# Where the value products of the band pairs stand in TensorE's order: odd pairs first in their turn, even pairs last

## The chip, the cores and the metric

The kernel runs on one core of a Trainium2 chip. The core has a matrix engine (TensorE, PE in the profile; its weight loads are shown as PEld), VectorE (DVE), ScalarE (ACT), GpSimd (POOL) and a sync engine (SP) that issues most DMAs. Each engine works through its own queue, and the queues are tied together by semaphores. TensorE writes its results to PSUM, from where ACT and DVE read them. The metric is the time of one execution in device microseconds, as the median of several runs.

## What is computed

The reference is a two-layer encoder trunk on 1024 tokens of width 1024. Each layer has 16 attention heads of width 64 in three groups, an output projection and a gated feed-forward part. The change touches the attention of the groups A and B, whose scores lie in a band around the diagonal:

```python
for l in range(DEPTH):                                  # DEPTH = 2
    h = rms_norm(x, g_attn[l]) * (1 + sc_a) + sh_a
    qa, ka, va, qb, kb, vb, qc, kc, vc = split_cols(h @ w_in[l], IN_SPLITS)
    ya = neighborhood_attention(qa, ka, va, rpb_na[l])                   # 4 heads
    yb = sliding_window_attention(qb, kb, vb, sink_sw[l], t5_table)      # 6 heads
    yc = axial_attention(qc, kc, vc, gq_ax[l], gk_ax[l])                 # 6 heads, dense
    y = concat(rms_norm(ya, ga), rms_norm(yb, gb), rms_norm(yc, gc))
    x = x + gt_a * (y @ w_o[l])
    ...                                                  # feed-forward part

# sliding window, per 128-query block, against the 3 blocks of keys around it:
s = einsum('bnqgrd,bnkgd->bngrqk', qb, kb) * scale + bias
p = softmax(concat([s, sink_logits]))[..., :-1]
o = einsum('bngrqk,bnkgd->bnqgrd', p, vb)
```

## The kernel before

The attention of one layer is a stream of 64 pairs. A pair is one head with 256 queries (two blocks of 128), numbered p = 0 to 3 within a head. Pairs 0 to 23 are the dense group C (class `PairC`), pairs 24 to 39 are group A (`PairA`) and 40 to 63 are group B (`PairB`); A and B are both `Band`, and they are what the change touches.

A band pair goes through these steps:

- `scores` (line 1571): four products on TensorE into a PSUM tile (sA or sB in the profile; two buffers of two banks each), then two instructions on DVE that add the bias and take the maximum into `pr`.
- `exps` (line 1592): two exponentials on ACT, in place in `pr`.
- `divide` (line 1600): a reciprocal on DVE and two scalings on POOL.
- `turn` (line 1603): four transposes into one PSUM bank and one or two into another (both named T; three banks in all), then a cast on ACT of the first bank to the high part (`pt<-T`) and a copy of the second (`edge<-T`). `low` puts the low part together on DVE from the first bank (also `pt<-T,pt`).
- `pv` (line 1624): the value products, four with the two parts of `pt` and two or four hardware products with `edge`, into the PSUM tile pv.
- `fold` (line 1431) and `combine` (line 1440), for odd p only: ACT copies 64 rows of pv to the tile cmb, and DVE adds them to the other rows and writes y.

The pv tile holds two pairs: an even pair writes its left half and the odd pair after it the right half, and both are folded together. `psV` has `4 - PS_T` banks, and PS_T is 3, so there is one bank for pv (line 1361). An even pair therefore may not begin `pv` before `combine` of the odd pair ahead of it has read the bank.

The loop at line 1767 runs over turns n. In the band part (its last branch, line 1794) a turn works on several pairs at once: `divide` for n + 2, `low` of n - 1, `combine` of n - 3, `scores` of n + 4, `exps` of n + 3, `turn` of n, `pv` and `fold` of n - 2. Where this text says an odd or an even turn it means the parity of n, which is that of the pair whose `pv` and `turn` it holds. While `pin` is on (line 1876), TensorE, ACT, DVE and POOL keep exactly the order in which the code writes their instructions; the work in `later` and what stands below line 1822 (norm statistics, scalings of y, splits of the output projection's weights) is placed by the scheduler. All engine calls go through one helper, so that every row of the profile has its line, L49, and rows are told apart by their tiles.

Of the kernel before, what the change touches and what calls it, by code (L numbers as in the profile page):

```python
# [85 lines left out]
def trunk(ctx: ExitStack, tc, A, C, out):  # L86
# [5 lines left out]
    def pin(engines, on):  # L92
        for e in engines:
            e.pinned = on
# [103 lines left out]
    def w_rows(w, r0, hl=None, eng=None):  # L198

        return split_w(lambda v: [(v, w[r0 : r0 + P, :])], 1, hl, eng)  # L200
# [704 lines left out]
    for l in range(2):  # L905
# [14 lines left out]
        def qk_tile():  # L920
            return qkp.tile([P, 5, S], F32R, name="qk", tag="qk", bufs=2)
# [133 lines left out]
        def rows_A(i):  # L1055
            sp.dma_start(skA[i], bc(skr[4 * i : 4 * i + 4][:, None, :], [4, P, 512]))

        def rows_B():
            for h in range(6):
                sp.dma_start(skB[h], bc(rowB[h][None, :], [P, 512]))  # L1060
# [210 lines left out]
        def opened(p0, p1, p2, p3):  # L1271

            p0.turn(0)
            p2.dots(0)
            p0.turn(1)
            p2.dots(1)
            low = p1.turn_high(0, 0)
            p0.pv(0)
            p2.max(0)
            p2.exp(0)  # L1280
            low()
            low = p1.turn_high(0, 1)
            p0.pv(1)
            p2.max(1)
            low()
            low = p1.turn_high(1, 0)
            p2.exp(1)
            p3.dots(0)
            low()
            low = p1.turn_high(1, 1)  # L1290
            p1.pv(0)
            p3.max(0)
            unfinished.pop(0)()
            p3.exp(0)
            low()
            p3.dots(1)
            p1.pv(1, False)
            p1.fold()
            p3.max(1)
            p3.exp(1)  # L1300
            p1.combine()
# [172 lines left out]
        class PairC(Pair):  # L1474
# [8 lines left out]
            def max(self, c):  # L1483
                c_max(self.s[c], c, self.rs)
# [217 lines left out]
        def y_split(k, half, hi, lo):  # L1702

            c = slice(half * H, (half + 1) * H)
            g = vec[:, 64 + k : 65 + k]
            act.activation(hi, y[:, k, c], AF.Copy, scale=g)
            dve.scalar_tensor_tensor(
                out=lo, in0=y[:, k, c], scalar=g, in1=f32(hi), op0=ALU.mult, op1=ALU.subtract
            )
# [6 lines left out]
        def w_o_stage(k):  # L1716
            st = stage()
            sp.dma_start(st, w_o[k * P : (k + 1) * P, :])
            return st

        def o_rows(ki, w, ns):
            wh, wl = w
            if ki < 5:
                hi, lo = yq[:, ki, 0:H], yq[:, ki, H:S]
            else:
                hi, lo = yb[0][:, ki - 5, :], yb[1][:, ki - 5, :]
            for n in ns:
                cs = slice(n * P, (n + 1) * P)
                mm3(pss[n], wh[:, cs], wl[:, cs], hi, lo, ki == 0, ki == 7)
# [31 lines left out]
        N = len(stream)  # L1761
        pairs = {}
        AHEAD, AHEAD_B, NC = 3, 4, 24
# [3 lines left out]
        for n in range(-AHEAD - 1, N + 3):  # L1767
            ahead = AHEAD if n + AHEAD < NC else AHEAD_B
            begin = range(done, min(n + ahead + 1, N))
            if n < 0:  # L1770
                begin = range(done, done)
            elif n == 0:
                opened(*(pairs[i] for i in range(4)))
                begin = range(3, 4)
                fresh = []
            elif n < NC:
                for i in range(2 if n > 1 else 0):
                    if 0 <= n:
                        pairs[n].turn(i)
                    while unfinished:  # L1780
                        unfinished.pop(0)()
                    if 2 <= n - 1:
                        pairs[n - 1].pv(i)
                    for m in begin:
                        if m < min(made, NC):
                            pairs[m].qk(i)
                for i in range(2 if n == 1 else 0):
                    pairs[begin[0]].qk(i)
                fresh = [pairs[m] for m in begin if NC <= m < made]
                for b in fresh:  # L1790
                    b.scores()
                    b.exps()
                    b.divide()
            else:
                for b in worked:
                    b.divide()
                if NC <= n - 1 < N:
                    pairs[n - 1].low()
                if NC <= n - 3:
                    pairs[n - 3].combine()  # L1800
                fresh = [pairs[m] for m in begin if m < made]
                for b in fresh:
                    b.scores()
                for b in scored:
                    b.exps()
                if n < N:
                    pairs[n].turn()
                if NC <= n - 2 < N:
                    pairs[n - 2].pv()
                    pairs[n - 2].fold()  # L1810
                elif n == NC:
                    for i in range(2):
                        pairs[n - 1].pv(i)
                scored, worked = fresh, scored
            done = max(done, min(begin.stop, made)) if n >= 0 else done
            while made < min(N, n + ahead + 2):
                for key, make in preload.get(made, []):
                    heads[key] = make()
                pairs[made] = stream[made][0]()
                made += 1  # L1820
            if n >= 0:
                pin((pe, act, dve), False)
            for what in later.pop(n, []):
                what()
            if n in (0, 6):
                for j in range(8):
                    (v_back if n else v_store)(j)
            if n == 4 and l == 0:
                rows_A(1)
                rows_B()  # L1830
            if n == 6:
                pin((sp,), False)
            if n == 50:
                yq = qk_tile()
            if n == 54:
                wst = [w_o_stage(k) for k in korder[:2]]
            if n in (55, 59):
                ki = (n - 55) // 4
                y_split(korder[ki], 0, yq[:, ki, 0:H], yq[:, ki, H:S])
            if n in (59, 61):  # L1840
                w01.append(split_tile(wst.pop(0), 1, (atp, "pr", 6), dve))
            if n == 60:
                t2 = [psS.tile([P, 2, H], F32, name="ps_o", tag="S") for _ in range(2)]
                pss = [t2[i // 2][:, i % 2, :] for i in range(NS)]
            if n in (61, 62):
                o_rows(0, w01[0], range(NS)[2 * (n - 61) : 2 * (n - 60)])
            if n in (63, 64):
                o_rows(1, w01[1], range(NS)[2 * (n - 63) : 2 * (n - 62)])
            if n == 62:
                wq = [w_rows(w_o, k * P, eng=dve) for k in korder[2:4]]  # L1850
            m = n - 1 if n <= NC else n - 3
            for end, (chunks, width) in norms.items():
                if begins[end] <= m <= end and (m - begins[end]) % 8 == 7 and (n <= NC or m >= NC):
                    i = (m - begins[end]) // 8
                    if end not in gss:
                        gss[end] = gss_tile()
                    for half in range(2):
                        what = lambda a=(chunks, gss[end], i, half, m == N - 1): norm_sum(*a)
                        if m == N - 1:
                            what()  # L1860
                        else:
                            later.setdefault(n + 1 + half, []).append(what)
                    if m == end and end < N - 1:

                        def stats(end=end, width=width, n=n, chunks=chunks):
                            r = rstd_cols([gss[end]], width, 8, atp, psT, tag="T", newton=True)

                            def scale():
                                todo = norm_scale(chunks, r, psT, "T", (pool, pool))
                                for i, what in enumerate(todo):  # L1870
                                    later.setdefault(n + 9 + i, []).append(what)

                            later.setdefault(n + 8, []).append(scale)

                        later.setdefault(n + 5, []).append(stats)
            pin((pe, act, dve), n < 0 or n >= NC - 1)
# [713 lines left out]
```

## Time and profile before

| what | value |
|---|---|
| median of 3 runs | 2369.87 us (2369.44 to 2372.74) |
| the profiled execution's own time | 2368.57 us |
| its span | 2366.8 us |
| granted TensorE clock, mean | 0.998 |
| instructions | 33472 |
| first and last product into pv | 232.2 and 1628.0 us |
| VectorE, ScalarE, GpSimd: share of the span busy | 74%, 50%, 33% |

The bands of layer 0 run from about 359 to 454 us of the span and those of layer 1 from about 1549 to 1632 us. A row of the view in order of time reads: start in us, duration in us (of all instructions merged into the row), engine, line, operation, output<-inputs with shapes, count, and in brackets how long the engine had been idle before it and which instruction ended that. A row of the waits reads: who waited, for what, us in total, how many times, and the longest.

### The profile page before, as it was taken

What the parts mean: (1) busy time and instruction counts of PE and PEld (TensorE: products, weight loads), DVE (VectorE), ACT (ScalarE), POOL (GpSimd) and SP (SyncE); (2) the same over time, 40 slices, a digit from 0 to 9 for tenths busy, and PEclk for the clock granted to TensorE, in tenths of its full rate; (3) what the DMA queues carried; (4) which work ended last, traced back from release to release, by engine and by line L of the source; (5) the groups of instructions that cost most, each with busy time, mean ns of one, the idle gap of its engine ahead of it and who ended that gap; (6) DMA issues with size and microseconds to landing.
All of it is one profiled execution on the core that took longest, in us unless ns stands there. A gap on an engine that the chain in (4) does not pass through costs nothing. (4 is left out here: it accounts for less than half of the span.)

```text
span 2366.8 us, 33472 instructions
## 1 busy us (share of the span) xinstructions
PE 2325.0 (98%) x11804; PEld 1959.9 (83%) x11804; DVE 1756.6 (74%) x2753; ACT 1184.7 (50%) x2261; POOL 775.7 (33%) x747
## 2 busy tenths in 40 slices
PE   9999999999999999999999999999999999999998
PEld 7888898888788888788888889988878888888886
DVE  6877998869867677595767789897796674537765
ACT  4423888845543333344633168896454434334443
POOL 1530447610344445100145124574005444430001
PEclk9999999999999999999999999999999999999999
DMA  8667416162434444775434861332634443239633
GB/s 280 182 207 227 127 27 192 44 217 94 138 130 165 156 138 151 217 245 175 155 100 133 247 186 28 92 103 94 218 98 132 154 150 103 98 106 299 209 120 112
DMA packets 307417, 358.02 MB, mean 151 GB/s; under 512 B 51996, under 2 KB 223868, under 8 KB 307248
## 3 DMA queue, kind: packets, MB, share of 16 engines
q1 hardware_dynamic: 290752, 346.26, 46.4%
q10 hardware_dynamic: 16128, 9.44, 1.5%
q8 instruction: 93, 1.52, 0.3%
q14 instruction: 76, 0.62, 0.1%
q0 software_dynamic: 368, 0.17, 0.0%
HBM read 270.84 MB, written 88.63 MB: 152 GB/s over the span
## 5 line engine op out<-in xcount | busy, mean ns | idle before, releaser
L49 PE MATMUL ps_d<-wpt 128*128 128x512 f32 x1848 | 423.8, 390 | 1.0 <-ACT wpt L49 0.7
L49 PEld LDWEIGHTS ps_d<-wpt 128*128 128x128 f32 x1848 | 345.7, 188 | 74.4 <-issue 3.0
L49 POOL TENSOR_SCALAR pr<-pr,rs 128x1024 f32<-128x1024 f32 (+2 forms) x248 | 190.3, 780 | 186.2 <-DVE rs L49 169.7
L49 POOL TENSOR_TENSOR sg<-sg,u 128x512 f32<-128x512 f32 x82 | 118.0, 1440 | 348.4 <-ACT sg L49 221.6
L49 PE MATMUL pv<-pt,vs 128*128 128x256 f32 x1088 | 173.9, 296 | 14.6 <-DVE y L49 13.3
L49 DVE TENSOR_TENSOR pt<-T,pt 128x512 fp32r<-128x512 f32 x272 | 177.4, 680 | 7.0 <-ACT pt L49 5.9
L49 ACT CAST wpt<-w 128x512 fp32r<-128x512 f32 x154 | 95.7, 621 | 173.5 <-PE ps_d L49 155.3
L49 DVE SCALAR_TENSOR_TENSOR acc<-wmt,condT,acc 128x512 f32<-128x512 f32 (+1 forms) x98 | 117.0, 1202 | 77.7 <-DMA wmt<-in_w_mod_dram 77.2
L49 ACT CAST pt<-T 128x512 fp32r<-128x512 f32 x272 | 151.5, 585 | 42.0 <-PE T L49 40.7
L49 ACT COPY u<-ps_w 128x512 f32<-128x512 f32 x128 | 75.1, 586 | 192.9 <-PE ps_w L49 192.9
L49 POOL TENSOR_TENSOR wpt<-ws,wpt 128x512 fp32r<-128x512 f32 x80 | 111.2, 1390 | 182.2 <-ACT wpt L49 137.2
L49 DVE TENSOR_TENSOR wpt<-w,wpt 128x512 fp32r<-128x512 f32 x154 | 108.9, 707 | 79.2 <-ACT wpt L49 76.9
L49 PEld LDWEIGHTS pv<-pt,vs 128*128 128x128 f32 x1088 | 141.0, 189 | 27.2 <-DVE y L49 25.2
L49 PE MATMUL T<-identr,pr 128*128 128x128 f32 x1176 | 160.1, 273 | 0.9 <-ACT edge L49 0.5
L49 PEld LDWEIGHTS T<-identr,pr 128*128 128x128 f32 x1176 | 137.7, 140 | 16.0 <-issue 1.4
L49 ACT CAST wpt<-ws 128x512 fp32r<-128x512 f32 x176 | 107.7, 622 | 52.9 <-issue 22.9
L49 DVE TENSOR_TENSOR wpt<-graw,wpt 128x512 fp32r<-128x512 f32 x154 | 109.8, 713 | 16.6 <-ACT wpt L49 16.4
L49 ACT CAST wpt<-graw 128x512 fp32r<-128x512 f32 x154 | 95.0, 617 | 52.7 <-DMA graw<-gpd 43.6
L49 DVE TENSOR_TENSOR wpt<-ws,wpt 128x512 fp32r<-128x512 f32 x96 | 82.7, 869 | 49.3 <-ACT wpt L49 49.1
L49 DVE TENSOR_TENSOR ws<-wr 128x512 f32<-128x512 f32 x88 | 81.2, 923 | 50.0 <-POOL wpt L49 46.6
L49 DVE TENSOR_REDUCE rs<-sC 128x1 f32<-128x1024 f32 x88 | 107.4, 1221 | 12.7 <-PE sC L49 11.4
L49 PE MATMUL ps_w<-ht3h,wpt 128*128 128x512 f32 x352 | 108.8, 390 | 2.4 <-ACT sg L49 2.4
(306 smaller groups left out, 5931.5 us busy)
## 6 DMA issues: line engine op xcount, KB each, us to landing
wr<-in_w_gu_dram SPq DMA_DIRECT2D x92, 512.0 KB, 4.2
gpd<-sg SPq DMA_DIRECT2D x154, 256.0 KB, 4.4
graw<-gpd SPq DMA_DIRECT2D x76, 512.0 KB, 3.5
w<-in_w_down_dram SPq DMA_DIRECT2D x110, 256.0 KB, 5.4
wmt<-in_w_mod_dram SPq DMA_DIRECT2D x48, 512.0 KB, 5.9
qk<-qkd SPq DMA_DIRECT2D x44, 512.0 KB, 7.2
wst<-in_w_o_dram SPq DMA_DIRECT2D x32, 512.0 KB, 4.4
wmt<-in_w_mod_dram SPq DMA_DIRECT2D x64, 256.0 KB, 3.9
```

Source lines behind the costliest of these rows:

```text
L49: ins = op(*args, **kwargs)
```

## The change

In the band branch of the loop the pair whose value products belong to the turn (n - 2) is now called `ready`. If its p is odd, its `pv` is called ahead of the turn's scores; if its p is even, after the turn's transposes as before. `fold` is called where it was. Nothing else differs.

```diff
                 fresh = [pairs[m] for m in begin if m < made]
+                ready = pairs[n - 2] if NC <= n - 2 < N else None
+                if ready and ready.p % 2:
+                    ready.pv()
                 for b in fresh:
                     b.scores()
                 for b in scored:
                     b.exps()
                 if n < N:
                     pairs[n].turn()
-                if NC <= n - 2 < N:
-                    pairs[n - 2].pv()
-                    pairs[n - 2].fold()
+                if ready:
+                    if ready.p % 2 == 0:
+                        ready.pv()
+                    ready.fold()
                 elif n == NC:
                     for i in range(2):
                         pairs[n - 1].pv(i)
```

On TensorE, in the first head of group B in layer 0 (T are transposes, sB scores, pv value products), four turns read before:

```order
L49 MATMUL T<-identr,pr 128x128 x6
L49 MATMUL pv<-pt,vs 128x256 x4
L49 MATMUL pv<-edge,vs 128x128
L49 MATMUL sB<-qk 128x384 x4
L49 MATMUL T<-identr,pr 128x128 x6
L49 MATMUL pv<-pt,vs 128x256 x4
L49 MATMUL pv<-edge,vs 128x128
L49 MATMUL sB<-qk 128x384 x2
L49 MATMUL sB<-qk 128x256 x2
L49 MATMUL T<-identr,pr 128x128 x5
L49 MATMUL pv<-pt,vs 128x256 x4
L49 MATMUL pv<-edge,vs 128x128 x2
```

Every set of transposes is followed by one pair's value products: those of p = 3 (of the head before), p = 0 and p = 1 here.

The same place on TensorE after the change:

```order
L49 MATMUL pv<-pt,vs 128x256 x4
L49 MATMUL pv<-edge,vs 128x128
L49 MATMUL sB<-qk 128x384 x4
L49 MATMUL T<-identr,pr 128x128 x6
L49 MATMUL sB<-qk 128x384 x4
L49 MATMUL T<-identr,pr 128x128 x6
L49 MATMUL pv<-pt,vs 128x256 x4
L49 MATMUL pv<-edge,vs 128x128
L49 MATMUL pv<-pt,vs 128x256 x4
L49 MATMUL pv<-edge,vs 128x128 x2
L49 MATMUL sB<-qk 128x384 x2
L49 MATMUL sB<-qk 128x256 x2
```

The products of p = 3 moved ahead of the scores and transposes of their turn, and those of p = 1 directly behind those of p = 0, so that two turns' scores and transposes follow one another with no value product between them.

On ACT, in group B of layer 0, with the copy cmb of `fold` in an odd turn, the rows read the same before and after the change:

```order
L49 ACTIVATE pr,rs<-pr,rs 128x385
L49 CAST pt<-T 128x2x2x128
L49 COPY edge<-T 128x256
L49 COPY cmb<-pv 64x512
L49 ACTIVATE pr,rs<-pr,rs 128x385 x2
L49 CAST pt<-T 128x2x2x128
L49 COPY edge<-T 128x256
```

Nothing moved here: the copy cmb stands behind the cast and the edge copy of its turn in both.

## Prediction

> **What bounds the kernel now.** I read the busy shares first, then the groups with the most idle time, then the waits in the two stretches in which the bands run, and last the instructions of four turns in order of time.
>
> ```profile
> PE 2325.0 (98%) x11804; PEld 1959.9 (83%) x11804; DVE 1756.6 (74%) x2753; ACT 1184.7 (50%) x2261; POOL 775.7 (33%) x747
> L49 PEld LDWEIGHTS pv<-pt,vs 128*128 128x128 f32 x1088 | 141.0, 189 | 27.2 <-DVE y L49 25.2
> PEld pv L49 <- DVE y L49: 9.8, 14, 1.6
> PEld pv L49 <- DVE y L49: 9.5, 13, 1.6
> 400.00:450.00 50.00, 45.48 (x352) 42.97 (x351) 46.43 (x145) 47.59 (x136) 41.03 (x74) 1.00 0.14 47
> ```
>
> TensorE (PE) is busy for 98% of the span, so the span moves with PE's idle time and with little else. The largest idle time in front of the value products pv is the weight load's 25.2 us for y, which is `combine` on VectorE (DVE). The third and fourth lines give the share of the bands: 9.8 us in 359 to 454 us (layer 0) and 9.5 us in 1549 to 1632 us (layer 1), together 19.3 us. That is the most which any order of the band turns can win here. The last line is 50 us of bands (columns: PE, PEld, DVE, ACT, POOL busy, then clock). ScalarE (ACT) with 47.59 us and DVE with 46.43 us are as full as PE, so what a product waits for is set by how these two queues get through, and not by one slow instruction.
>
> Two turns follow in order of time. In the first (pair p = 1 of a head) PE does the odd product last; the next even product (409.03) is the one that waits; the first row is the even product one pair of turns earlier.
>
> ```profile
> 404.32 0.54 PEld L49 LDWEIGHTS pv<-pt,vs 128*128 128x128 f32 x4 [0.73 <-DVE y L49]
> 406.06 0.82 PE L49 MATMUL T<-identr,pr 128*128 128x128 f32 x6
> 406.63 0.72 PE L49 MATMUL pv<-pt,vs 128*128 128x256 f32 x4
> 406.69 0.59 ACT L49 CAST pt<-T 128x512 fp32r<-128x512 f32 x1 [0.28 <-PE T L49]
> 407.18 0.38 ACT L49 COPY edge<-T 128x256 f32<-128x256 f32 x1
> 407.33 0.96 PE L49 MATMUL sB<-qk 128*128 128x384 f32 x4
> 407.67 0.58 ACT L49 COPY cmb<-pv 64x512 f32<-64x512 f32 x1
> 408.13 0.82 PE L49 MATMUL T<-identr,pr 128*128 128x128 f32 x6
> 408.28 0.69 DVE L49 TENSOR_TENSOR y<-pv,cmb 64x512 f32<-64x512 f32 x1 [0.19 <-ACT cmb L49]
> 409.03 0.54 PEld L49 LDWEIGHTS pv<-pt,vs 128*128 128x128 f32 x4 [0.32 <-DVE y L49]
> ```
>
> There is one PSUM bank for pv. The even product may not open it until `combine` has read the pair before, `combine` needs the copy cmb (`fold`), and cmb stands on ACT behind the cast and the edge copy of the same turn. So there is a chain from the turn's first transpose: 406.06 (T) to 406.69 (cast), 407.18 (edge), 407.67 (cmb), 408.28 (y), 409.03 (pv), in steps of 0.63, 0.49, 0.49, 0.61 and 0.75 us: 2.97 us. In the cast's row ACT had been idle for 0.28 us and waited for T, so this chain really hangs on T. Meanwhile PE has 0.57 of transposes (406.06 to 406.63), 0.70 of odd product (to 407.33), 0.80 of scores (to 408.13) and 0.57 of transposes again: 2.64 us. The rest, 2.97 - 2.64 = 0.33 us, is the stall, and the row says 0.32.
>
> The other kind of turn, p = 3:
>
> ```profile
> 410.42 0.71 PE L49 MATMUL T<-identr,pr 128*128 128x128 f32 x5
> 410.83 0.61 ACT L49 ACTIVATE pr<-pr,rs 128x385 f32<-128x385 f32 x1
> 410.88 0.72 PE L49 MATMUL pv<-pt,vs 128*128 128x256 f32 x4
> 411.43 0.57 ACT L49 CAST pt<-T 128x512 fp32r<-128x512 f32 x1
> 411.80 0.83 PE L49 MATMUL sB<-qk 128*128 128x256 f32 x4
> 411.89 0.27 ACT L49 COPY edge<-T 128x128 f32<-128x128 f32 x1
> 412.19 0.58 ACT L49 COPY cmb<-pv 64x512 f32<-64x512 f32 x1
> 412.47 0.71 PE L49 MATMUL T<-identr,pr 128*128 128x128 f32 x5
> 412.81 0.68 DVE L49 TENSOR_TENSOR y<-pv,cmb 64x512 f32<-64x512 f32 x1
> 413.54 0.53 PEld L49 LDWEIGHTS pv<-pt,vs 128*128 128x128 f32 x4 [0.60 <-DVE y L49]
> ```
>
> Here the cast starts only 1.01 us after T, because ACT is still at an exponential (410.83). The steps are 1.01, 0.46, 0.30, 0.62 and 0.73: 3.12 us. PE covers 0.46 + 0.92 + 0.67 + 0.46 = 2.51 us of it, and 0.61 is left; the row says 0.60.
>
> **The change part by part.** No instruction is added or removed. The odd product goes from the end of its turn, behind T, to the turn's start, ahead of the scores. The even product stays last. `fold` keeps its place on ACT behind the cast and the edge copy, and `combine` its place on DVE in the turn after. So the start of the chain (T of the odd turn) and its end (the next turn's even product) are what they were, every link stays, and the odd product no longer lies between them: it has gone ahead of T.
>
> That the copy's data will be ready earlier does not help as long as ACT takes its queue in order. The trace has a case in which the data was ready and the copy did not start:
>
> ```profile
> 426.77 0.39 PE L49 MATMUL pv<-edge,vs 128*128 128x128 f32 x2
> 427.19 0.74 ACT L49 ACTIVATE qk<-y,vecs 128x512 fp32r<-128x512 f32 x1
> 427.95 0.58 ACT L49 COPY cmb<-pv 64x512 f32<-64x512 f32 x1
> 429.85 0.53 PEld L49 LDWEIGHTS pv<-pt,vs 128*128 128x128 f32 x4 [1.57 <-DVE y L49]
> ```
>
> The product ended at 426.77 + 0.39 = 427.16, and cmb began at 427.95, when the instruction queued ahead of it was through. [...]
>
> After p = 1 the cover falls to 0.57 + 0.80 + 0.57 = 1.94 us against the same 2.97: a stall of 1.03 in place of 0.33, so **+0.70 us**, the odd product itself. After p = 3 the cover falls to 0.46 + 0.67 + 0.46 = 1.59. If ACT is still behind, the chain is 3.12, the stall 1.53, and the cost the whole 0.92. If it is not, the cast starts 0.63 after T as in the first turn, the chain is 0.63 + 0.46 + 0.30 + 0.62 + 0.73 = 2.74, the stall 1.15, and the cost 1.15 - 0.61 = **0.54 us**. I take 0.54: two turns now last about 4.6 us (409.03 to 413.54 is 4.51, the pair of turns from 404.32 on 4.71) and would grow to 5.2, while ACT's 47.59 busy of 50 us is at most 4.4 per two turns of today, so ACT should have caught up by the time T ends. DVE could be late as well; in this steady stretch it is not:
>
> ```profile
> 407.42 0.67 DVE L49 TENSOR_TENSOR pt<-T,pt 128x512 fp32r<-128x512 f32 x1
> 409.01 0.62 DVE L49 CUSTOM_DVE_ANT_0 pr<-sB,bz,sinkc 128x384 f32<-128x384 f32 x1
> ```
>
> The low part needs the cast's end (406.69 + 0.59 = 407.28), `combine` stands behind it, and 407.42 + 0.67 = 408.09 is still ahead of 408.28; in the changed order this comes no later against T. The scores that stand behind `combine` on DVE (409.01) belong to a pair that PE transposes four turns later, so a delay of theirs does not come back to PE soon.
>
> How many turns: 19 even pairs a layer follow an odd band pair (numbers 26 to 62). Those in which something else covers the chain do not count:
>
> ```profile
> 377.38 1.84 PE L49 MATMUL ps_st<-onesr,gss 128*128 128x1 f32 x16
> 380.47 0.72 PE L49 MATMUL pv<-pt,vs 128*128 128x256 f32 x4
> 1617.32 0.47 PE L49 MATMUL ps_o<-qk,whi 128*128 128x512 f32 x1
> 1619.68 0.74 PE L49 MATMUL pv<-pt,vs 128*128 128x256 f32 x4 [0.45 <-DVE y L49]
> ```
>
> Twice a layer the statistics' products (ps_st, 1.84 us) lie between an odd turn's T and the even product; the one at 380.47 waits for nothing, and 1.94 + 1.84 is more than 2.97, so it should wait for nothing after the change either. Near the end (pairs 58, 60, 62) the output projection (ps_o) lies there, and I count nothing. That leaves 19 - 2 - 3 = 14, seven of each kind: 7 × 0.70 + 7 × 0.54 = 8.7 us a layer, **17.4 us** for two layers. Bounds: below, without the two disturbed turns of each layer (such as the one at 429.85, where other work on ACT and DVE sets the wait, so that cover may not matter), 12 × 0.62 × 2 = 14.9, and less if the copies start sooner than I think; above, all 19 turns at the whole odd product, 19 × 0.81 × 2 = 30.8.
>
> Of other edits: what the scheduler may move freely (statistics, scaling of y, splits of the output weights) changes places by a few rows on ACT, DVE and SP. I cost that at nothing, since these have a turn or more of stock; without that cover it is about one 0.74 us ACT instruction in a chain, two or three times a layer, some 3 us in all.
>
> The profiled execution took 2368.57 us (span 2366.8 and 1.8 around it), 1.3 below the median of 2369.87. 2368.57 + 17.4 = 2386.0; against the median 2387.3, and I forecast **2387 us**.
>
> **Rivals.** *Faster: the early product frees the copy.* If ACT reaches `fold` as soon as the odd product is done, ahead of T's cast, cmb and `combine` (0.61 + 0.75 us) lie under scores and transposes of two turns, more than 2.6 us, and all 19.3 us of waits go: 2350 us. It decides from the point at which T to pv is shorter than the cover of 1.94 or 1.59. For it: the product is ready more than a microsecond earlier. Against it: the order on ACT keeps the cast and the edge copy ahead, and so does DVE with the low part, and the row at 427.95. *No change.* The lost cover is made good by ACT having caught up: the chain after p = 3 would have to shrink from 3.12 by 0.92, and that after p = 1 from 2.97 by 0.70. The second cannot, as its cast already waits for T, so it needs half of the turns to hang on other work than T; then +0 to +6 us are left: 2370 to 2376. *Worse than forecast.* ACT stays behind in the p = 3 turns and the disturbed turns lose their whole cover too, or two sets of transposes in a row (with no product between them) wait for the T banks, which the low part and the edge copy free: the upper bound, 2369.87 + 30.8 = 2401 us. For it: three T banks, two taken in each turn, and now PE comes back for them 0.7 to 0.9 us sooner.
>
> **How the numbers follow.** Forecast (+10 to +25 us) 0.70; worse (over +25) 0.15; the near-nothing case 0.08, of which half lies within 0.2% (4.7 us, about what a measurement of this kernel can tell from no change); faster 0.07. So faster by over 0.2% 0.07, within 0.04, slower 0.89. The forecast's own range is 2380 to 2395; for 8 in 10 the range goes from 2376 to 2401, which leaves out the fast case, the near-nothing case and the far end.
>
> **What would show it.** In the changed profile the rows of PEld pv waiting for DVE y in the two stretches should sum to about 36 us in place of 19.3, with single waits near 1.0 and 1.15 in the steady turns of group B; a head of four turns should take about 10.5 us in place of 9.3 (404.32 to 413.54 is 9.22); cmb should follow the edge copy by 0.3 to 0.5 us as now, long after the odd product's end; ACT and DVE should be less than 90% busy in the bands, and PE's busy time the same. Wrong would be: waits for y gone (first rival), cmb ahead of the cast, ACT casts still starting 1 us after T (the costlier kind), or transposes waiting for low parts or edge copies in every turn.

## The result, and the profile after

| | before | after |
|---|---|---|
| median, us | 2370.29 (2369.44 to 2372.74, 6 runs) | 2385.99 (2384.8 to 2388.18, 6 runs) |
| profiled execution, us | 2368.57 | 2386.25 |
| its span, us | 2366.8 | 2384.5 |
| first sA to last pv, layer 0 | 359.0 to 470.5: 111.5 | 360.3 to 480.3: 120.0 |
| of it PE busy | 103.30 | 104.86 |
| first sA to last pv, layer 1 | 1507.5 to 1628.0: 120.5 | 1516.0 to 1646.1: 130.1 |
| of it PE busy | 112.59 | 115.89 |

The changed kernel takes 1.0067 times as long (95%: 1.0056 to 1.0077), 15.7 us more between the medians and 17.7 us between the profiled executions. The rows on the layers go by the starts of the first group A scores and of the last value product in each layer: the band parts grew by 8.5 and 9.6 us, 18.1 together, and the rest of the program gave 0.4 back. So all of the time is in the stretches that the change touches. (They are longer than the ones given ahead of the prediction, 359 to 454 and 1549 to 1632 us: layer 1's first group A scores start at 1507.5.) PE's idle time in them grew from 8.2 + 7.9 = 16.1 us to 15.1 + 14.2 = 29.3, by 13.2. The other 4.9 us are PE's busy time. About 1.3 of it is other work: in each layer 36 products of the output projection (ps_o) stand ahead of the last value product where there were 33. In layer 1, 3.41 us at half the granted clock add an estimated 1.7 (the next section has the rows). What the remaining 1.9 are, the profile does not say.

The changed kernel's page, with its busy shares and the value products' weight loads (columns: busy us, mean ns of one, idle before them), then the waits of the two band stretches (359 to 466 and 1555 to 1660 us), then 50 us of steady bands (busy time of PE, PEld, DVE, ACT and POOL, then the granted clock):

```profile
PE 2330.8 (98%) x11804; PEld 1964.0 (82%) x11804; DVE 1754.8 (74%) x2753; ACT 1187.2 (50%) x2261; POOL 774.0 (32%) x747
L49 PEld LDWEIGHTS pv<-pt,vs 128*128 128x128 f32 x1088 | 141.5, 190 | 37.3 <-DVE y L49 34.3
...
PEld pv L49 <- DVE y L49: 15.7, 16, 1.5
...
PEld pv L49 <- DVE y L49: 13.9, 14, 1.5
...
405.00:455.00 50.00, 40.86 (x313) 38.08 (x311) 41.99 (x128) 43.61 (x122) 37.20 (x67) 1.00 0.09 25
```

What grew most is the idle time ahead of the value products: 27.2 to 37.3 us on the page, of it 25.2 to 34.3 for y. In the band stretches it is 15.7 + 13.9 = 29.6 us in place of 19.3, and over the whole band parts of the table 15.9 + 15.2 = 31.1 in place of 11.2 + 10.8 = 22.0. In the steady 50 us PE's busy time falls from 45.48 to 40.86, and ACT and DVE fall with it (95% to 87%, 93% to 84%): the engines wait for each other longer. The clock column reads 1.00 here, as before.

The two kinds of turn, in order of time, in the same head as in the prediction. First p = 1:

```profile
410.40 0.39 PE L49 MATMUL pv<-edge,vs 128*128 128x128 f32 x2
411.33 0.82 PE L49 MATMUL T<-identr,pr 128*128 128x128 f32 x6
411.96 0.59 ACT L49 CAST pt<-T 128x512 fp32r<-128x512 f32 x1 [0.89 <-PE T L49]
412.45 0.38 ACT L49 COPY edge<-T 128x256 f32<-128x256 f32 x1
412.85 0.58 ACT L49 COPY cmb<-pv 64x512 f32<-64x512 f32 x1
413.46 0.69 DVE L49 TENSOR_TENSOR y<-pv,cmb 64x512 f32<-64x512 f32 x1
414.21 0.53 PEld L49 LDWEIGHTS pv<-pt,vs 128*128 128x128 f32 x4 [0.94 <-DVE y L49]
```

The odd product is done at 410.40 + 0.39 = 410.79, and cmb, which needs nothing else, starts at 412.85, after ACT has waited 0.89 us for T and then done the cast and the edge copy. From T to the next even product the steps are 0.63, 0.49, 0.40, 0.61 and 0.75: 2.88 us against a cover of 1.94, and 0.94 is left, as the row says. And p = 3:

```profile
416.52 0.71 PE L49 MATMUL T<-identr,pr 128*128 128x128 f32 x5
417.15 0.59 ACT L49 CAST pt<-T 128x512 fp32r<-128x512 f32 x1 [0.45 <-PE T L49]
417.63 0.27 ACT L49 COPY edge<-T 128x128 f32<-128x128 f32 x1
417.93 0.58 ACT L49 COPY cmb<-pv 64x512 f32<-64x512 f32 x1
418.55 0.68 DVE L49 TENSOR_TENSOR y<-pv,cmb 64x512 f32<-64x512 f32 x1
419.28 0.53 PEld L49 LDWEIGHTS pv<-pt,vs 128*128 128x128 f32 x4 [1.16 <-DVE y L49]
```

ACT has caught up: it idled 0.45 us for T, and the cast starts 0.63 after T and not 1.01. The chain is 0.63 + 0.48 + 0.30 + 0.62 + 0.73 = 2.76, less the cover of 1.59 is 1.17. The idle time ahead of the product is 1.16.

### The profile page after: what moved, and what is told of

Same layout as the page of the kernel before. It is cut to its first block, busy times and chain, and to the rows that moved or that the text cites. A ratio compares the mean times of both kernels' runs of the same rounds, so it can differ in the third digit from the quotient of the medians.

```text
span 2384.5 us, 33431 instructions
## 1 busy us (share of the span) xinstructions
PE 2330.8 (98%) x11804; PEld 1964.0 (82%) x11804; DVE 1754.8 (74%) x2753; ACT 1187.2 (50%) x2261; POOL 774.0 (32%) x747
## 4 chain that ended last, share of the span: by engine, by line
PE 53%; DVE 5%; issue 4%; DMA 3%; ACT 1%; POOL 1%; SPq 0%; POOLq 0%; DVEq 0%; ACTq 0%
PE ps_w L49 23%; PE ps_d L49 15%; PE ps_o L49 4%; PE pv L49 3%; PE ps_ab L49 3%; PE T L49 2%; DMA wmt<-in_w_mod_dram 2%; PE sC L49 2%; DVE ws L49 1%; DVE acc L49 1%; PE ps_c L49 1%; DVE wpt L49 1%; DMA graw<-gpd 0%; POOL ct L49 0%; DMA qk<-qkd 0%
## 5 line engine op out<-in xcount | busy, mean ns | idle before, releaser
L49 PEld LDWEIGHTS pv<-pt,vs 128*128 128x128 f32 x1088 | 141.5, 190 | 37.3 <-DVE y L49 34.3
L49 PE MATMUL ps_w<-h22h,wpt 128*128 128x512 f32 x352 | 109.0, 391 | 2.5 <-ACT u L49 1.5
```

The lines of the kernel that those rows point to most:

```text
L49: ins = op(*args, **kwargs)
```

## Where the extra time lies, turn by turn

The starts of the even products in both profiles give the extra time of each pair of turns (the step from one even product to the next, after less before; us, layer 0 / layer 1):

| even pairs | extra | predicted a layer |
|---|---|---|
| 34 to 44, steady | 3.41 / 3.39 | 3 × 0.54 + 3 × 0.70 = 3.72 |
| 26, 30, 32 | 1.24 / 1.19 | 1.78 |
| 28, 46 (ps_st turns) | 1.13 / 1.15 | 0 |
| 48, 50 | 1.27 / 1.28 | 1.24 |
| 52, 54, 56 | 1.31 / 2.61 | 1.94 |
| 58, 60, 62 (end) | 0.11 / 0.02 | 0 |
| sum | 8.5 / 9.6 | 8.7 |

The steady turns carry the mechanism cleanly: 0.61 after p = 1 and 0.56 to 0.58 after p = 3 (0.42 to 0.45 at pair 38, whose product waited 0.73 and not 0.60 before). In the others it mixes with what the scheduler placed, and two of those are worth reading. A ps_st turn of the changed kernel:

```profile
380.78 0.17 DVE L49 TENSOR_SCALAR isq<-ps_st 128x8 f32<-128x8 f32 x1 [1.18 <-PE ps_st L49]
380.93 0.67 DVE L49 TENSOR_TENSOR pt<-T,pt 128x512 fp32r<-128x512 f32 x1
381.59 0.67 DVE L49 TENSOR_TENSOR y<-pv,cmb 64x512 f32<-64x512 f32 x1
382.32 0.54 PEld L49 LDWEIGHTS pv<-pt,vs 128*128 128x128 f32 x4 [0.35 <-DVE y L49]
```

The prediction took the 1.84 us of ps_st as cover. But here a DVE instruction that reads ps_st stands ahead of the low part and `combine`, so the cover delays the very chain that it was to cover: DVE waits 1.18 us, and the product 0.35. In the kernel before, the low part of that turn stood ahead of the reader of ps_st, which came at 379.27:

```profile
377.38 0.67 DVE L49 TENSOR_TENSOR pt<-T,pt 128x512 fp32r<-128x512 f32 x1
```

And pair 50, which costs 1.34:

```profile
441.89 0.72 ACT L49 ACTIVATE qk<-y,vecs 128x512 fp32r<-128x512 f32 x1 [1.81 <-POOL y L49]
442.52 0.57 ACT L49 CAST pt<-T 128x512 fp32r<-128x512 f32 x1
443.31 0.14 PEld L49 LDWEIGHTS T<-identr,pr 128*128 128x128 f32 x1 [1.72 <-ACT edge L49]
```

Here ACT idled 1.81 us ahead of one instruction that waits for GpSimd, with the turn's cast queued behind it, and the transposes then waited 1.72 us for the edge copy.

Pair 52, right behind it, costs 0.20 us in layer 0 and 1.62 in layer 1, though the code is the same for both layers. The difference of 1.4 us comes with the granted clock (in odd_mid the pair costs 0.18 and 0.03). Two stretches of layer 1 in the changed kernel, each 3.41 us long (busy time of PE, PEld, DVE, ACT and POOL, then the clock), and a set of scores in the second one:

```profile
1606.65:1610.06 3.41, 1.37 (x10) 1.18 (x11) 2.46 (x8) 3.36 (x11) 3.41 (x6) 1.00 0.22 58
1610.06:1613.47 3.41, 3.41 (x17) 3.31 (x16) 1.93 (x5) 1.77 (x6) 3.41 (x5) 0.50 0.00 0
```

```profile
1611.16 1.63 PE L49 MATMUL sB<-qk 128*128 128x384 f32 x4
```

The four products took 1.63 us, and 0.96 in the row at 407.33 that the prediction shows. Ahead of that stretch PE had been busy for 1.37 of 3.41 us, 40%: pair 50's waits fall there.

In the profile of the changed kernel this is the one place in the band parts at which the clock falls; in that of the kernel before there is none (1.00 from 16.8 to 2358.3 us). Such a fall is not the change's alone: over 405 to 455 us fold_early reads 0.97, where the change and only_p3 read 1.00. A pause of PE by itself does not tell when it comes: at the same turn of layer 0 PE was busy for 0.94 us of the 3.41 from 441.22 on, 28%, and the clock stayed at 1.00. No run was made to find what brings it.

## The experiments

All times are medians beside runs of the kernel before on the same chip. In the three groups of runs the kernel before took 2371.28 (2367.99 to 2374.83; for fold_early, fold_combine_early, only_p3 and only_p1), 2371.24 (2367.63 to 2375.21; for combine_first, cmb_alone and late_even) and 2370.95 us (2366.77 to 2376.46; for odd_mid and late_even_56), and ratios are to that. An ellipsis marks what is left out of a diff. The theory: the odd product was cover between an odd turn's transposes and the next even product, and two queues that are worked off in order, ACT (cast and edge copy ahead of `fold`) and DVE (low part ahead of `combine`), keep the chain where it was. The change's profile shows this order on both: ahead of 441.89 ACT idled 1.81 us although the transposes that the cast behind it reads were over at 440.10 + 0.71 = 440.81, and ahead of 380.78 DVE idled 1.18 us although the cast that the low part behind it reads was over at 378.88 + 0.58 = 379.46.

| kernel | edit, against | us | ratio (95%) |
|---|---|---|---|
| the change | before | 2385.99 | 1.0067 (1.0056 to 1.0077) |
| fold_early | change | 2384.06 (2383.26 to 2389.16) | 1.0059 (1.0047 to 1.0072) |
| fold_combine_early | change | 2376.43 (2372.41 to 2377.5) | 1.0019 (1.0009 to 1.003) |
| combine_first | change | 2391.78 (2389.2 to 2393.87) | 1.0087 (1.0072 to 1.0102) |
| only_p3 | change | 2384.91 (2380.73 to 2386.99) | 1.0057 (1.0045 to 1.007) |
| only_p1 | change | 2380.98 (2378.49 to 2381.23) | 1.0041 (1.0029 to 1.0054) |
| cmb_alone | change | 2378.5 (2377.84 to 2382.03) | 1.0036 (1.0023 to 1.0049) |
| odd_mid | change | 2385.16 (2382.45 to 2386.56) | 1.0053 (1.004 to 1.0066) |
| late_even | before | 2369.68 (2366.23 to 2375.28) | 0.9995 (0.9985 to 1.0005) |
| late_even_56 | before | 2367.85 (2366.75 to 2371.31) | 0.9986 (0.9977 to 0.9995) |

### ACT's queue alone: the copy ahead of the cast

```diff
                 for b in scored:
                     b.exps()
+                if ready and ready.p % 2:
+                    ready.fold()
                 if n < N:
                     pairs[n].turn()
                 if ready:
                     if ready.p % 2 == 0:
                         ready.pv()
-                    ready.fold()
```

> The changed kernel, but fold (the copy cmb) stands on ACT behind the exponentials and ahead of the turn's cast. Theory (the chain T, cast, edge copy, cmb, combine, even product sets the wait, and DVE's low part is the next link): cmb starts about 1 us earlier, but combine still stands behind low on DVE and low needs the cast, so combine begins only about 0.16 us earlier (in the changed kernel low starts at 412.69 and combine at 413.46; low's 0.61 us pitch allows 413.30). About 34 turns x 0.16 = 5 us off: 2379 to 2386 us, and the waits of PEld pv for y stay above 20 us in the bands. Rival (ACT's order alone holds the early product back): the waits for y go, about 30 us off: 2350 to 2360 us.

It took 1.9 us less than the change, with ranges that overlap. A p = 3 turn of this kernel, in order of time:

```profile
418.99 0.58 ACT L49 COPY cmb<-pv 64x512 f32<-64x512 f32 x1
...
419.28 0.71 PE L49 MATMUL T<-identr,pr 128*128 128x128 f32 x5
419.91 0.59 ACT L49 CAST pt<-T 128x512 fp32r<-128x512 f32 x1 [0.34 <-PE T L49]
...
420.53 0.69 DVE L49 TENSOR_TENSOR pt<-T,pt 128x512 fp32r<-128x512 f32 x1
421.14 0.67 DVE L49 TENSOR_TENSOR y<-pv,cmb 64x512 f32<-64x512 f32 x1
421.87 0.54 PEld L49 LDWEIGHTS pv<-pt,vs 128*128 128x128 f32 x4 [0.99 <-DVE y L49]
```

The copy is now ahead of the cast, as it was meant to be, and is through at 419.57. `combine` starts at 421.14 all the same, because the low part is ahead of it on DVE and needs the cast. That is a second chain from T: 0.63 + 0.62 + 0.61 + 0.73 = 2.59 us, beside the 2.76 that the change has over ACT (in one turn, that of pair 38, it is 2.73). The steady stalls are 0.73 to 0.88 us after p = 1 and 0.98 to 1.13 after p = 3, in place of 0.94 and 1.16: 0.03 to 0.21 us less, where 0.16 a turn were expected. Two ways of nearly equal length lead from the transposes to the next product, and taking one away leaves the other.

### Both queues: copy and sum ahead of the cast and the low part

```diff
-                if NC <= n - 3:
-                    pairs[n - 3].combine()
...
+                if ready and ready.p % 2:
+                    ready.fold()
+                    ready.combine()
                 if n < N:
                     pairs[n].turn()
```

> The changed kernel, but fold stands on ACT ahead of the turn's cast and combine on DVE in the same odd turn, behind that turn's two score instructions and ahead of the next turn's low. Theory: the waits of the even product for y nearly go (under 6 us in the bands instead of 30), but low comes 0.5 to 0.6 us later, and the edge transposes of the next turn need the T bank that low frees; they now wait 0.6 to 0.8 us in each even turn, so the time stays within 6 us of the changed kernel's 2386: 2380 to 2391 us, with PE T waiting for DVE pt in nearly every even turn. Rival (the pv bank is the only thing that the early product waits for): no new wait, 2350 to 2360 us.

This lies between the two ranges that were expected, below the theory's and above the rival's. Its waits (360 to 480 us), then a stretch in order of time:

```profile
PEld pv L49 <- DVE y L49: 4.3, 9, 0.7
PEld T L49 <- ACT edge L49: 4.2, 8, 0.9
```

```profile
408.95 0.82 PE L49 MATMUL T<-identr,pr 128*128 128x128 f32 x6
409.12 0.58 ACT L49 COPY cmb<-pv 64x512 f32<-64x512 f32 x1
...
410.30 0.81 PE L49 MATMUL T<-identr,pr 128*128 128x128 f32 x6
410.34 0.69 DVE L49 TENSOR_TENSOR y<-pv,cmb 64x512 f32<-64x512 f32 x1
411.09 0.53 PEld L49 LDWEIGHTS pv<-pt,vs 128*128 128x128 f32 x4 [0.21 <-DVE y L49]
411.27 0.69 DVE L49 TENSOR_TENSOR pt<-T,pt 128x512 fp32r<-128x512 f32 x1
```

With both queues out of the way the wait for y falls to 4.3 us in layer 0 (over the whole band part, 359 to 484 us, it is 11.2 before and 15.9 in the change), and the product waits 0.21. A steady head takes 411.09 to 419.86 = 8.77 us, against 9.21 before and 10.38 in the change, all three from the even product of pair 40 to that of pair 44. I had expected the transposes to wait for the low part, which is now late. They don't: the row at 410.30 is over at 411.11, before the low part of 411.27 begins. New waits of the transposes, for the edge copy (4.2 us) and for GpSimd's scaled scores (3.2), take back part of it, and so do the turns with scheduler-placed work and the end of the bands (pair 62 costs 3.4 us more than before in layer 1 and 5.0 in layer 0; the profiled run's mean granted clock is 0.995, beside 0.998 in the kernel before). In all it is 9.6 us faster than the change and still slower than before.

### DVE's queue alone: the sum ahead of the low part

```diff
-                if NC <= n - 1 < N:
-                    pairs[n - 1].low()
                 if NC <= n - 3:
                     pairs[n - 3].combine()
+                if NC <= n - 1 < N:
+                    pairs[n - 1].low()
```

> The changed kernel, but combine stands on DVE ahead of low; fold as in the change. Theory (two queues hold the even product, each of them alone is enough): cmb still stands behind cast and edge copy, so combine begins when it did; within 3 us of the changed kernel (2383 to 2389 us), although fold_combine_early, with both moved, took off about 10. Rival (fold_combine_early won by combine's place alone): 2375 to 2379 us.

The waits for y, the wait on the copy, and one `combine`, of layer 0:

```profile
PEld pv L49 <- DVE y L49: 18.5, 18, 1.3
...
DVE y L49 <- ACT cmb L49: 10.4, 14, 1.1
```

```profile
411.62 0.69 DVE L49 TENSOR_TENSOR y<-pv,cmb 64x512 f32<-64x512 f32 x1 [0.72 <-ACT cmb L49]
```

`combine` is early in its queue and stands there waiting for cmb, 0.72 us in this row. The steady stalls are 0.94 and 1.16, as in the change. The total is 3 us above the range that was expected. In the profile the ps_st turns of layer 0 lost another 0.5 us each (pairs 28 and 46), and pair 52 costs 1.5 and 2.5 us. The profiled run's mean granted clock is 0.994, beside 0.997 in the change. The mean granted clock of the four runs is 0.9955, beside 0.9968 in the fifteen of the kernel before, which over 2390 us would be 3 us (an estimate). So each queue alone holds the product, and both together, as in the kernel above, let it go.

### Half the change: only p = 3, only p = 1

```diff
-                if ready and ready.p % 2:
+                if ready and ready.p == 3:
                     ready.pv()
...
-                    if ready.p % 2 == 0:
+                    if ready.p != 3:
                         ready.pv()
```

> Only the products of p = 3 stand first in their turn; those of p = 1 stand last as before. Theory (each early odd product takes its own time out of the cover of the next even one): 8 to 9 turns a layer at about 0.6 us, 7 to 10 us above before: 2377 to 2381 us, the even products of p = 0 waiting about 0.95 us and those of p = 2 about 0.6 as before. Rival (the cost comes from two sets of transposes that follow one another in every pair of turns, or from ACT and DVE as a whole): not half of the cost; either nothing (2370) or nearly all of it (2385).

The other has 1 in place of 3.

> Only the products of p = 1 stand first in their turn; those of p = 3 stand last as before. Theory: the other half, 6 to 10 us above before: 2376 to 2381 us, the even products of p = 2 waiting about 1.15 us and those of p = 0 about 0.33 as before; only_p3 and only_p1 together add up to the change's 15.7 us within 4. Rival: the parts do not add up (each costs nearly all or nothing).

The even products of two successive pairs of turns, in order of time, first of only_p3, then of only_p1:

```profile
405.44 0.54 PEld L49 LDWEIGHTS pv<-pt,vs 128*128 128x128 f32 x4 [0.93 <-DVE y L49]
...
409.99 0.53 PEld L49 LDWEIGHTS pv<-pt,vs 128*128 128x128 f32 x4 [0.64 <-DVE y L49]
```

```profile
408.51 0.53 PEld L49 LDWEIGHTS pv<-pt,vs 128*128 128x128 f32 x4 [1.17 <-DVE y L49]
...
413.21 0.53 PEld L49 LDWEIGHTS pv<-pt,vs 128*128 128x128 f32 x4 [0.33 <-DVE y L49]
```

Each half changes only its own kind of wait: 0.93 in the first, beside 0.64 (0.60 to 0.73 before), and 1.17 in the second, beside an untouched 0.33 (0.32 before). The product of p = 3 is that of n - 2, so it stood behind the transposes of a p = 1 turn: only_p3 therefore lengthens the wait that was 0.32, and only_p1 the one that was 0.60. Over the pairs 32 to 44 the two halves cost 2.34 + 1.55 = 3.9 us of layer 0, and the whole change 3.58.

In total they don't add up: 13.6 + 9.7 = 23.3 us against 15.7. The total of only_p3 missed its range and came out where its rival had it, at nearly the whole cost, and the sum missed the 4 us that were allowed; only the steady turns went as the theory says. The profiles show two things in the excess. One is the clock: its mean is 0.994 in both profiled runs, beside 0.997 in the change. The mean clock of only_p1's five runs is 0.9946, beside 0.9962 in the kernel before, an estimated 3.8 us of its 9.7; only_p3's is 0.9960. The other is the turns with scheduler-placed work (layer 0; only_p3: pairs 46 and 52 at 1.0 and 1.1, with a clock of 1.00 over 405 to 455 us; only_p1: pair 50 at 1.55, with 1.04 back at 48). In only_p3's pair 60 (1.31) and only_p1's pair 52 (2.25) the two are not told apart. I read that from the profiles; no run takes either away.

### The bank freed by the copy alone

cmb is added to itself, so half of the bands' value products are left out of y, and DVE no longer reads the pv bank:

```diff
                 a, b = self.pvt[r0 : r0 + 64], self.t[r0 : r0 + 64]
+                if isinstance(self, Band):
+                    a = b
```

> The changed kernel, but combine of the band pairs adds the copy cmb to itself and does not read the pv tile (half of the value products is left out of y); instructions, sizes and queues are the same. Theory (the even product waits for the bank, which combine is the last to read): the bank is now free when cmb is done, 0.7 us earlier; stalls of about 0.2 us (p = 0) and 0.45 us (p = 2) in place of 0.94 and 1.16, so about 34 x 0.7 = 24 us off the changed kernel: 2360 to 2366 us, with the waits of PEld pv for y replaced by waits for cmb. Rival (two sets of transposes in a row, or the load of ACT and DVE, cost the time, and the wait for the bank only shows it): within 5 us of 2386.

The waits of layer 0's bands, and a steady even product:

```profile
PEld pv L49 <- ACT cmb L49: 5.3, 14, 0.5
```

```profile
415.64 0.53 PEld L49 LDWEIGHTS pv<-pt,vs 128*128 128x128 f32 x4 [0.47 <-ACT cmb L49]
```

The product's releaser changes from y to cmb, which shows that it is the bank that it waits for. What stays is the copy's own place behind cast and edge copy. The total fell by 7.5 us, not by the 20 or more that were expected, and by more than the 5 of the rival: the band parts were 7.1 and 7.9 us ahead of the change by pair 58, but the transposes came to wait for GpSimd (4.1 us in layer 0) and the edge copy (2.8), and the last two even pairs gave 3.5 us a layer back.

### Where the odd product stands ahead of the transposes

```diff
-                if ready and ready.p % 2:
-                    ready.pv()
                 for b in fresh:
                     b.scores()
+                if ready and ready.p % 2:
+                    ready.pv()
```

> The changed kernel, but the odd products stand between the scores and the transposes of their turn, not ahead of the scores. Theory (only what lies between an odd turn's transposes and the next even product is cover): the scores change sides of the odd product, but both stay ahead of T, so the cover is the same 1.94 and 1.59 us and the time within 3 us of the change in the steady turns and within 5 in all: 2382 to 2391 us, stalls near 0.94 and 1.16 us. Rival (the cost comes from standing first in the turn, ahead of the scores, which makes scores and bias late): 2372 to 2378 us.

In order of time:

```profile
411.13 0.82 PE L49 MATMUL T<-identr,pr 128*128 128x128 f32 x6
...
414.01 0.54 PEld L49 LDWEIGHTS pv<-pt,vs 128*128 128x128 f32 x4 [0.95 <-DVE y L49]
```

414.01 - 411.13 is the 2.88 us of the change again, and the stall is 0.95 where the change has 0.94. The odd product ends a set of scores later, and in the steady turns nothing changes: it is of no account when the odd product's data is ready, only whether it lies between the transposes and the next even product.

### The opposite edit: more cover

The odd product is left where it was before, and the even one goes behind the scores of the next turn:

```diff
                 for b in fresh:
                     b.scores()
+                if n % 2 and NC <= n - 3 < N:
+                    pairs[n - 3].pv()
                 for b in scored:
                     b.exps()
                 if n < N:
                     pairs[n].turn()
                 if NC <= n - 2 < N:
-                    pairs[n - 2].pv()
-                    pairs[n - 2].fold()
+                    if n % 2:
+                        pairs[n - 2].pv()
+                        pairs[n - 2].fold()
```

> The kernel before, but the even products are moved the other way: later, behind the scores of the next turn; odd products, fold and combine as before. Theory (cover of the chain decides): the chain of 2.97 or 3.12 us from an odd turn's first transpose now has 2.64 + 0.67 = 3.31 or 2.51 + 0.80 = 3.31 us of PE work over it, so the waits for y nearly go in the steady turns (0.94 us per head of four turns) and ACT, 8.4 us of work per head, becomes the bound: 0.8 us per head, 8 to 9 heads per layer, 12 to 16 us faster than before: 2354 to 2359 us. Rival (ACT and DVE bind already, and the wait for y only shows it): the waits go elsewhere and the time stays within 4 us of before.

In the steady turns it does what the theory says: a head takes 409.04 to 417.58 = 8.54 us in place of 9.21, and by pair 58 the layers are 3.4 and 3.0 us ahead of the kernel before, counted from the first scores of the bands. Yet the total is the same within its interval, and not the 2354 to 2359 us that were expected. The turns of pairs 38, 46, 50 and 54 cost 0.3 to 0.6 more each, and at pair 60 of layer 0, in order of time:

```profile
458.34 2.30 DVE L49 TENSOR_TENSOR wlo<-wst,whi 128x1024 fp32r<-128x1024 f32 x1
460.56 0.68 DVE L49 TENSOR_TENSOR pt<-T,pt 128x512 fp32r<-128x512 f32 x1
461.16 0.67 DVE L49 TENSOR_TENSOR y<-pv,cmb 64x512 f32<-64x512 f32 x1
461.88 0.53 PEld L49 LDWEIGHTS pv<-pt,vs 128*128 128x128 f32 x4 [1.87 <-DVE y L49]
```

A split of the output projection's weights, 2.30 us on DVE, stands ahead of the low part and `combine`, and takes 1.9 us back. At the last value product 1.6 and 1.3 us are left. The last run keeps the old order from pair 57 on:

```diff
-                if n % 2 and NC <= n - 3 < N:
+                if n % 2 and NC <= n - 3 <= 56:
...
-                    if n % 2:
+                    if n % 2 or n - 2 > 56:
```

> late_even, but only up to pair 56; the last three even pairs of a layer, whose turns share DVE and ACT with the split of the output weights, keep the order of before. Theory (late_even gains about 0.3 us a turn in the steady part, 4 us a layer by pair 58, and gives 1.9 of it back at pair 60): 4 to 9 us faster than before, 2362 to 2367 us. Rival (the end of the bands is set by the split of the output weights on DVE, so what is gained ahead of it is lost there in whatever order): within 3 us of before, 2367 to 2374 us.

It is 3.1 us faster than before, 0.9986 (0.9977 to 0.9995), the fastest median found, and less of a gain than the theory gave: the time is in the rival's range. The product of pair 60 still waits in it, 1.89 us ahead of 461.18. So the order of the value products at the end was not the reason for that wait. What a split placed elsewhere would bring was not tried.

## Why the prediction was right, point by point

- **Forecast.** 17.4 us were predicted and 15.7 measured (17.7 between the profiled executions), as slower, inside the range. That the sum came so close is in part luck: in the profile the 14 turns that were counted cost 7.2 and 8.5 us a layer, 1.4 of it by the clock, and 2.3 us for both layers came from turns that were counted at nothing.
- **The chain stays, the cover goes.** Shown: T to even product takes 2.88 and 2.76 us against 2.97 and 2.74 predicted, the covers 1.94 and 1.59 are what they were worked out to be, and moving the odd product about ahead of the transposes (odd_mid) changes nothing in the steady turns. The product waits for the bank (cmb_alone), and with both queues shortened (fold_combine_early) that wait falls to 4.3 us in layer 0, so it is the chain to the bank's last reader, and not PE, that holds the product.
- **The p = 1 term, +0.70, was too high: 0.61.** The step from the edge copy to cmb was taken as 0.49 from the profile of before. But there the end of the odd product came last, in a row that the prediction does not have (kernel before, in order of time):

```profile
407.19 0.38 PE L49 MATMUL pv<-edge,vs 128*128 128x128 f32 x2
```

  It ends at 407.57, 0.10 ahead of cmb's 407.67. With that product done long before, cmb follows the edge copy at 0.40, which takes 0.09 off chain and stall. That was to be had from the trace of before.
- **The p = 3 term, +0.54, was right: 0.56.** ACT had caught up, as assumed; the cast starts 0.63 after T.
- **The 14 turns.** Right as a sum, not as a list. The ps_st turns were counted at nothing and cost 1.1 us a layer; the pairs 26, 30 and 32 cost 0.6 less than was counted. The ps_st step failed because it looked at PE's row only. Work that fills PE's time is cover only if nothing in the chain's own queues waits for that work, as DVE did here for 1.18 us.
- **Scheduler-placed work at nothing (3 us at most).** It moved single pairs by up to 0.8 us against their terms (pair 50 above at 1.34 for 0.54, pair 52 at 0.20 for 0.70 in layer 0), and in the change this came out even. That 52 to 56 cost 2.61 in layer 1 and 1.31 in layer 0 goes with the clock, 0.50 for 3.41 us from 1610.06 on, for which the prediction had no term. In the half changes the two together cost 7.6 us beyond the change's own time.
- **The signs.** A head of four turns takes 408.89 to 419.28 = 10.39 us (10.5 predicted), ACT and DVE are below 90% busy, and no T of the steady turns waits for a low part.
- **Waits for y of about 36 us: 29.6.** Over the whole band parts they grew by 9.1 of the 18.1 us, from 22.0 and not from 19.3. The time came, but some of it stands under other names: transposes that wait for the edge copy (2.3 us in each layer against 0.5 and 0.6 before, over the whole band parts), and PE's busy time, which was to stay the same and is 4.9 us longer, for the reasons in the first section as far as they are known. The rival with the fast copy fell in fold_early, where the copy is early and the product is not.

What stays open is why one order of the value products costs up to 1 us more than another in the turns that hold scheduler-placed work. The rows show which queue is late there, but no run took that work out or put it elsewhere. How much of each median is due to the clock is an estimate as well.

## What to carry to other kernels

Cover is to be counted between the start of a chain and its end in the waiting engine's own order: moving work that was ready anyway to a place ahead of the chain's start can cost nearly all of its time (here 0.61 of 0.70 us and 0.56 of 0.92), though nothing was added and its data comes earlier. When a result passes through the queues of two engines that are worked off in order (here a cast stood behind an idle ACT for 1.81 us, a low part behind an idle DVE for 1.18), look for every way from start to end: here there were two of 2.59 and 2.76 us, and only both edits at once gave a gain clear of the spread. Before a steady-state gain is summed up, walk through the turns in which other work shares those queues: late_even was 3 us a layer ahead at pair 58, kept half of it to the end of the bands, and its total can't be told from the kernel before. And when the same turn costs more in one layer than in the other, look at the clock there (here 0.50 for 3.41 us) before a queue is blamed.

## What was not expected of the hardware

The granted clock read 1.00 in the steady bands although PE's products waited 0.70 and 0.93 us in every second turn (at 414.21 and 419.28). But in layer 1 of the changed kernel it was 0.50 for 3.41 us, after 3.41 us in which PE had been busy for 40%, and not in layer 0 after 28%, and four score products took 1.63 us in place of 0.96. The size of one head-of-queue wait was new to me: ACT did nothing for 1.81 us, with a cast behind it whose transposes had been over for 1.08 us, because one instruction waited for GpSimd.
